# Other buffers for down weights, token tiles and forget gates, and a later place for the queries' weight splits, in a hybrid decoder layer

## The chip, the cores and the metric

The kernel runs on one core of one Trainium2 chip. The metric is the device time of one execution in microseconds; the median of the runs counts. The engines of the core are TensorE (PE in the profile, its weight loads PEld), VectorE (DVE), ScalarE (ACT), GpSimd (POOL) and SyncE (SP), on whose queue all the DMAs named here are issued. Each engine runs its instructions in the order in which they stand in its queue.

## The reference

One layer of a decoder trunk over 1024 tokens with 1024 channels, float32 in and out. Cut to what matters:

```python
x = x + 0.5 * swiglu(rms_norm(x, ffn1_norm), ffn1_w_gate, ffn1_w_up, ffn1_w_down)   # hidden 2816
h = rms_norm(x, mix_norm)
(q_lat, kv_lat, k_rope, fq, fk, fv, f_logit, g_mla, g_fox) = split(h @ w_in)
y_mla = mla_mixer(q_lat, kv_lat, k_rope, ...)           # low-rank latents, rotary key, 8 heads
log_f = log_sigmoid(f_logit + b_f); c = cumsum(log_f)   # forget gates of the 8 FoX heads
y_fox = blocked_causal_attention(norm(fq), norm(fk), fv, bias=c[t] - c[s])
mixed = sigmoid(g_mla + b0) * (y_mla @ w_branch_mla) + sigmoid(g_fox + b1) * (y_fox @ w_branch_fox)
x = x + mixed @ w_o
x = x + 0.5 * swiglu(rms_norm(x, ffn2_norm), ffn2_w_gate, ffn2_w_up, ffn2_w_down)
```

## The kernel before

Matrix products run on PE in float16 with each operand split into a high and a low part, and three products in place of one (hi*hi, hi*lo, lo*hi). The split is made by `split_sb`: ACT writes the high part (L165), DVE the low part (L166). Nearly every operand that PE reads has gone through these two lines.

Both FFNs use a scheme of seven products for a 2x2 block product. In the **up projection** (`ffn_up`, matmuls at L1010) the 22 columns of 128 of the hidden layer are done as two first tiles and then pair tiles, numbered up to 21; POOL makes sums of the weights and activations (L985 to L999, L1060), and after each odd pair `act_sums` (POOL, L826) makes the sums of activations that the down projection needs, which go to DRAM (`sumd`, written at L830). The **down projection** (`ffn_down`, matmuls at L1169 into `psd`) has 70 steps n = (c, i, k): two halves c, seven products i, and CK = 5 blocks k each. A step's operands are prepared three steps ahead by `prep`: it reads the activations' sum back from DRAM (L1109), splits it and the weight (L165, L166), and for four of the products POOL first makes a difference of weight blocks (`made`, L1141: t1, t2, t3, t4). The weight blocks are loaded by `down_load` (L914). `load_x` (L508) loads the eight token tiles to which the result is added; DVE adds it when PSUM is evicted (L1177). `pending` is the `act_sums` of the last pair; it is called at step n = 2*CK.

Behind FFN1 the **tail** (`tail(t)`, called during the end of FFN1's down projection and after it) takes token tile by token tile: normalise it (y, L597), transpose it on PE (L604), split it into high and low (L612 on ACT, L625 on DVE), and project it onto the latents (`lat`, 360 columns: MLA's latents and the forget logits), which are written to DRAM (`latd`, L1299). Then comes the **in-projection** (`in_proj`, `proj_steps`): FoX q, k and v in three groups of weights of 1024x512, each loaded in four pieces by `in_weights` (L1280, into the two buffers `stgi`) and split (L165 to `s_wd`, L166 to `s_act`). Steps of MLA's projections and of the forget gates stand between the tiles. For q and k, `fox_qk` normalises each tile over heads (L1366 to L1371) and transposes it (`psft`, L1376). `forget` loads the logits from `latd` (`fg`, L1397), adds the bias `fb` (L1400), takes the log sigmoid and the running sum, and writes the sums split into high and low (`chl`, L1443 and L1444) to DRAM (`ad` and `bd`, L1446). Its tiles come from the ring of buffers with the tag `stg`, of which there are two and to which `stgi` belongs as well.

Big buffers come from a pool with four tags: 8 slots `u`, and 4 each of `v`, `act` and `wd`. A slot can be written again once its last reader is done, and a load stands on SP's queue until then, with all that is behind it. A scheduler sets the order of instructions on each engine from the program's order and its own costs; `follow` ties an instruction to one that must stand ahead of it in the order.

Of the kernel before, what the change touches and what calls it, by code (L numbers as in the profile page):

```python
# [18 lines left out]
P = 128  # L19
# [45 lines left out]
class Layer:  # L65
# [93 lines left out]
    def split_sb(self, hi, lo, src, scale=None):  # L159
# [4 lines left out]
        else:  # L164
            self.nc.scalar.activation(hi, src, AF.Copy, scale=scale)  # L165
            self.nc.vector.scalar_tensor_tensor(  # L166
                out=lo, in0=src, scalar=scale, in1=hi, op0=ALU.mult, op1=ALU.subtract
            )

# [88 lines left out]
    def layer(self):  # L258
# [18 lines left out]
        def tail(t):  # L277
# [9 lines left out]
            if t >= 1:  # L287
                for f in held.pop(0):
                    f()
            if t >= 2:  # L290
                self.lat_tile(lat["w"], mix, t - 2)
# [3 lines left out]
        x = self.parts("act", NT, 2)  # L295
        mix["x"] = x
        self.ffn_down(x, src, "ffn1", dict(raw=("u", "u"), extra="v", acts="wd", both=("v", "v")), tail, pending)
# [8 lines left out]
        self.in_proj(hT, gates)  # L306
# [453 lines left out]
    def up_tiles(self, norm, name, tags, loads, stats, scales, sumd):  # L760
# [4 lines left out]
        def tile(j, ops, tok, finish, mid):  # L765
# [7 lines left out]
            if j % 2:  # L773
                then = lambda a=box["even"], b=e, k=j // 2 - 1: self.act_sums(a, b, sumd[:, :, k, :], j == NH - 1)
# [300 lines left out]
    def ffn_down(self, x, old, name, tags, tail, pending):  # L1075
# [15 lines left out]
        def weights(k):  # L1091
            if k >= KT or k in raw:
                return
            w = self.down_load(name, k, self.slot(tags["raw"][k % 2]))
# [30 lines left out]
        def prep(n):  # L1125
# [13 lines left out]
            if i in made:  # L1139
                o, u, v = (w[s] for s in made[i])  # L1140
                nc.gpsimd.tensor_tensor(out=o, in0=u, in1=v, op=ALU.subtract)  # L1141
                if (c, i) == (0, 1):
                    second.append(self.latest(mybir.EngineType.Pool))
                if (c, i) == (0, 3):
                    self.follow(second[-1])
# [3 lines left out]
        second = []  # L1149
        mx = self.psa("mx")  # L1150
        ready = [prep(n) for n in range(ahead)]
        self.load_x(x, old, range(NT), loaded[1] if name == "ffn1" else None)
        for n, (c, i, k) in enumerate(steps):
# [8 lines left out]
            if n == 2 * CK:  # L1162
                pending()
# [100 lines left out]
    def in_weights(self, name, c0):  # L1264
# [7 lines left out]
        for kk in range(KD // 2):  # L1272
# [9 lines left out]
            self.split_sb(h, l, st, scale)  # L1282
# [18 lines left out]
    def in_proj(self, hT, gates):  # L1301
# [14 lines left out]
        with self.in_order(mybir.EngineType.PE):  # L1316
            self.proj_steps(hT, gates, groups, due, stages)

    def proj_steps(self, hT, gates, groups, due, stages):
        nc = self.nc  # L1320
        for h in range(2 * 3 * NT):
            gi, t, half = h // (2 * NT), h // 2 % NT, h % 2
            name, c0 = groups[gi]
            if t == 0 and half == 0:
                w = self.in_weights(name, c0)
# [63 lines left out]
    def forget(self):  # L1389
# [4 lines left out]
        w = self.ring.tile([P, 8, N], F32, tag="stg", bufs=2, name="fg")  # L1394
# [25 lines left out]
        to = self.ring.tile([P, 2, P], F32, tag="stg", bufs=2, name="tri")  # L1420
# [9 lines left out]
        ones = self.ring.tile([HEADS, T], F32, tag="stg", bufs=2, name="ones")  # L1430
# [4 lines left out]
        for n in range(2):  # L1435
# [4 lines left out]
            for sgn, dst, r0 in ((1.0, self.ad, 0), (-1.0, self.bd, 1)):  # L1440
                both = self.ring.tile([HEADS, 2, HALF], F32R, tag="stg", bufs=2, name="chl")
# [576 lines left out]
```

## Time and profile before

| | |
|---|---|
| time, three runs | 2097.16, 2098.95, 2099.48 us (median 2098.95) |
| profiled execution | 2101.86 us |
| its span | 2100.0 us, granted TensorE clock 0.992 on the mean |
| PE busy | 2049.2 us, 98% |
| DVE busy | 1445.1 us, 69% |
| ACT busy | 1171.3 us, 56% |
| POOL busy | 647.8 us, 31% |

In the rows of a timeline the first number is the start in us from the start of the span, the second the duration, then engine, line, operation, output<-input, shape and count; in brackets stands the idle time of the engine just ahead of it, and what ended it. FFN1's up projection ends at about 442 us, its down projection at about 640, the tail at 699, the in-projection's q, k and v at about 890; FFN2's down projection starts at about 1888.

### The profile page before, as it was taken

To read this page: it belongs to the slowest core of one execution; us is meant where nothing else is said; L and a number is where in the kernel's file an instruction comes from. 1 tells how busy PE (TensorE), PEld (TensorE's weight loads), DVE (VectorE), ACT (ScalarE), POOL (GpSimd) and SP (SyncE) were. 2 spreads that over 40 slices of the span, in tenths; PEclk is the share of its full clock that TensorE was granted. 3 is DMA by queue.
4 is the path that set the end of the run, shared out by engine and by line. 5 is a ranking of instruction groups with operands and counts; after the bars stand their busy time and mean duration, and the time that the engine had idled before them with its cause. 6 is when DMAs were issued, how large, how long until landed. Compare 5 with 4: busy or idle time off the path is not lost.

```text
span 2100.0 us, 28674 instructions
## 1 busy us (share of the span) xinstructions
PE 2049.2 (98%) x10239; PEld 1160.6 (55%) x10239; DVE 1445.1 (69%) x2421; ACT 1171.3 (56%) x1970; POOL 647.8 (31%) x719
## 2 busy tenths in 40 slices
PE   7999999999999998999999999999999999999999
PEld 4444444444446564567776668888544444444445
DVE  7856666679877776656667777864765555459886
ACT  7666665545554544456666765422566666554552
POOL 2455544463200111112222222000154555555300
PEclk9999999999999999999999999999999999999999
DMA  8258675365434456675555674551454564355432
GB/s 226 75 160 267 209 235 156 140 235 183 139 120 162 138 172 202 205 190 141 145 143 143 185 211 134 181 170 61 121 151 141 170 191 135 121 206 191 141 107 113
DMA packets 275288, 342.02 MB, mean 163 GB/s; under 512 B 20921, under 2 KB 205097, under 8 KB 275146
## 3 DMA queue, kind: packets, MB, share of 16 engines
q1 hardware_dynamic: 275146, 340.21, 52.5%
q8 instruction: 80, 1.31, 0.3%
q14 instruction: 62, 0.51, 0.1%
HBM read 242.15 MB, written 98.00 MB: 162 GB/s over the span
## 4 chain that ended last, share of the span: by engine, by line
PE 83%; DVE 8%; DMA 4%; ACT 3%; issue 2%; SPq 0%; POOL 0%; DVEq 0%; ACTq 0%; POOLq 0%
PE pst L1010 18%; PE psd L1169 15%; PE psb L1010 10%; PE psg L1010 3%; PE pss L1801 3%; PE pspt L1827 3%; PE psb L157 2%; PE psb L155 2%; PE psb L156 2%; PE pspv L1838 2%; PE psgate L155 2%; PE psgate L156 2%; PE psgate L157 2%; DVE op L166 2%; PE psin L156 1%
## 5 line engine op out<-in xcount | busy, mean ns | idle before, releaser
L1010 PEld LDWEIGHTS <-op 128*128 128x128 f16 x3360 | 328.7, 98 | 389.9 <-DVE s_act L1058 1.8
L1169 PE MATMUL psd<-op 128*128 128x512 f16 x1680 | 368.8, 382 | 8.9 <-DVE op L166 8.5
L1169 PEld LDWEIGHTS <-op 128*128 128x128 f16 x1680 | 165.2, 98 | 211.1 <-issue 11.0
L166 DVE SCALAR_TENSOR_TENSOR op<-s_u,s_v,op 128x512 f16<-128x512 f32 x170 | 150.1, 892 | 89.8 <-ACT op L165 89.3
L165 ACT ACTIVATE op<-s_u,s_v 128x512 f16<-128x512 f32 x170 | 118.0, 715 | 88.5 <-PE psd L1169 77.9
L1010 PE MATMUL pst<-s_u,op 128*128 128x512 f16 x720 | 165.2, 379 | 1.3 <-DVE s_act L1058 1.3
L1010 PE MATMUL pst<-s_v,op 128*128 128x512 f16 x720 | 165.2, 379 | 1.3 <-DVE s_u L1058 1.3
L1808 ACT ACTIVATE s_act<-pss,nm 128x128 f32<-128x128 f32 (+7 forms) x128 | 94.9, 742 | 95.1 <-DVE nm L1805 94.7
L166 DVE SCALAR_TENSOR_TENSOR op<-s_act,s_wd,op 128x512 f16<-128x512 f32 x100 | 91.7, 933 | 58.2 <-ACT op L165 58.2
L1848 POOL COPY atp<-cmb 64x128 f32<-64x128 f32 x64 | 18.4, 287 | 331.5 <-DVE cmb L1846 331.5
L1801 PE MATMUL pss<-s_wd 96*128 96x256 f32 (+5 forms) x480 | 115.1, 363 | 1.1 <-DMA s_wd<-mk 1.1
L985 POOL TENSOR_TENSOR sums<-s_u 128x512 f32<-128x512 f32 x20 | 25.8, 1291 | 252.6 <-PE psa L604 158.2
L1831 DVE TENSOR_TENSOR s_v<-pspt,s_v 128x512 fp32r<-128x512 f32 (+1 forms) x160 | 96.1, 631 | 9.9 <-ACT s_v L1830 8.5
L155 PE MATMUL psgate<-s_u,whi 128*128 128x512 f16 x256 | 97.6, 381 | 0.7 <-ACT z L1650 0.5
L157 PE MATMUL psgate<-s_u,wlo 128*128 128x512 f16 x256 | 97.1, 379 | 0.4 <-DVE wlo L166 0.4
L156 PE MATMUL psgate<-s_u,whi 128*128 128x512 f16 x256 | 97.1, 379 | 0.0
L165 ACT ACTIVATE op<-s_wd 128x512 f16<-128x512 f32 x70 | 50.1, 721 | 82.5 <-PE psd L1169 78.4
L1805 DVE TENSOR_REDUCE nm<-pss 128x1 f32<-128x128 f32 (+7 forms) x128 | 93.9, 751 | 1.6
L1830 ACT CAST s_v<-pspt 128x512 fp32r<-128x512 f32 (+1 forms) x160 | 81.3, 545 | 22.7 <-PE pspt L1827 21.3
L1827 PE MATMUL pspt<-ident,s_act 128*128 128x128 f32 x576 | 89.8, 278 | 3.7 <-ACT s_act L1808 2.5
L1846 DVE TENSOR_TENSOR cmb<-pspv,cmb 64x512 f32<-64x512 f32 x64 | 44.0, 688 | 69.8 <-ACT cmb L1845 69.3
L1010 PE MATMUL psb<-s_wd,op 128*128 128x512 f16 x360 | 82.6, 379 | 0.0
(550 smaller groups left out, 4664.6 us busy)
## 6 DMA issues: line engine op xcount, KB each, us to landing
sumd<-s_u SPq DMA_DIRECT2D x20, 1024.0 KB
s_wd<-in_ffn_w_down_dram SPq DMA_DIRECT2D x32, 512.0 KB
s_u<-in_w_in_dram SPq DMA_DIRECT2D x15, 1024.0 KB
sumd<-s_wd SPq DMA_DIRECT2D x13, 1024.0 KB
s_wd<-fd SPq DMA_DIRECT2D x48, 256.0 KB
s_u<-in_ffn_w_down_dram SPq DMA_DIRECT2D x22, 512.0 KB
s_wd<-sumd SPq DMA_DIRECT2D x14, 768.0 KB
s_u<-sumd SPq DMA_DIRECT2D x14, 768.0 KB
```

The lines of the kernel that those rows point to most:

```text
L155: mm(out, lhsT=lh, rhs=rh, start=start, stop=False)
L156: mm(out, lhsT=lh, rhs=rl, start=False, stop=False)
L157: mm(out, lhsT=ll, rhs=rh, start=False, stop=stop)
L165: self.nc.scalar.activation(hi, src, AF.Copy, scale=scale)
L166: self.nc.vector.scalar_tensor_tensor(out=lo, in0=src, scalar=scale, in1=hi, op0=ALU.mult, op1=ALU.subtract)
L1010: mm(out, lhsT=a[:, k, :], rhs=b[:, k, :], start=start and k == 0 and i == 0, stop=k == n - 1 and i == 2, skip_group_check=True,)
L1169: nc.tensor.matmul(o, lhsT=u[:, r], rhs=w, start=start and m == 0, stop=k == CK - 1 and m == 2, skip_group_check=True,)
L1801: mm(ps[:, b:e], lhsT=a[:, q], rhs=bb[:, b:e], start=k == 0, stop=k == len(passes) - 1)
L1805: nc.vector.tensor_reduce(out=nm, in_=ps[:, :n], op=ALU.max, axis=AX.X, negate=True)
L1808: nc.scalar.activation(pn[:, :n], ps[:, :n], AF.Exp, bias=nm, accum_out=rs[:, i, j:j + 1])
L1827: nc.tensor.transpose(pt[:, o:o + P], pr[m][:, kt * P:(kt + 1) * P], self.ident)
L1831: nc.vector.tensor_tensor(out=lo, in0=pt[:, s0:], in1=hi, op=ALU.subtract)
```

## The change

Five parts. (1) FFN1's ten down weight blocks go into `act` slots (0 to 3, 8 and 9; the up projection's weight pairs use these) and `u` slots (4 to 7) in turn, where they all used `u`; the token tiles of FFN1's down projection go into `u` slots, where the norm's output was, and not `act`; they are loaded behind weight block 4 and not behind block 1. (2) In both FFNs the rule that held the first t3 behind the last t2 on POOL is gone. (3) In FFN2 the last pair's `act_sums` are called at n = CK in place of 2*CK, without the tie on their last operation. (4) The splits of q's weights are tied behind the tail's tile 5 on ACT and DVE. (5) `forget` has its tiles in two `u` slots and not in the `stg` ring.

```diff
@@ split_sb
-    def split_sb(self, hi, lo, src, scale=None):
+    def split_sb(self, hi, lo, src, scale=None, after=()):
...
             self.nc.scalar.activation(hi, src, AF.Copy, scale=scale)
+            if after:
+                self.follow(after[0])
             self.nc.vector.scalar_tensor_tensor(
                 out=lo, in0=src, scalar=scale, in1=hi, op0=ALU.mult, op1=ALU.subtract
             )
+            if after:
+                self.follow(after[1])
@@ the program's order: tail, FFN1's down projection, in-projection
+            if t == 5:
+                lat["mark"] = [self.latest(e) for e in (mybir.EngineType.Activation, mybir.EngineType.DVE)]
...
-        x = self.parts("act", NT, 2)
+        x = self.parts("u", NT, 2)
...
-        self.ffn_down(x, src, "ffn1", dict(raw=("u", "u"), extra="v", acts="wd", both=("v", "v")), tail, pending)
+        self.ffn_down(x, src, "ffn1", dict(raw=("act",) * 4 + ("u",) * 4 + ("act",) * 2, extra="v", acts="wd", both=("v", "v")), tail, pending)
...
-        self.in_proj(hT, gates)
+        self.in_proj(hT, gates, lat["mark"])
@@ the up projection's last pair
-                then = lambda a=box["even"], b=e, k=j // 2 - 1: self.act_sums(a, b, sumd[:, :, k, :], j == NH - 1)
+                then = lambda a=box["even"], b=e, k=j // 2 - 1: self.act_sums(
+                    a, b, sumd[:, :, k, :], j == NH - 1 and name == "ffn1"
+                )
@@ ffn_down
-            w = self.down_load(name, k, self.slot(tags["raw"][k % 2]))
+            w = self.down_load(name, k, self.slot(tags["raw"][k % len(tags["raw"])]))
...
-                if (c, i) == (0, 1):
-                    second.append(self.latest(mybir.EngineType.Pool))
-                if (c, i) == (0, 3):
-                    self.follow(second[-1])
...
-        second = []
...
-        self.load_x(x, old, range(NT), loaded[1] if name == "ffn1" else None)
+        if name == "ffn2":
+            self.load_x(x, old, range(NT))
...
-            if n == 2 * CK:
+            if n == 1 and name == "ffn1":
+                self.load_x(x, old, range(NT), loaded[CK - 1])
+            if n == (2 * CK if name == "ffn1" else CK):
                 pending()
@@ in_weights and proj_steps
-    def in_weights(self, name, c0):
+    def in_weights(self, name, c0, after=()):
...
-            self.split_sb(h, l, st, scale)
+            self.split_sb(h, l, st, scale, after)
...
-                w = self.in_weights(name, c0)
+                w = self.in_weights(name, c0, mark if gi == 0 else ())
@@ forget
-        w = self.ring.tile([P, 8, N], F32, tag="stg", bufs=2, name="fg")
+        room, parts = self.slot("u"), self.slot("u", F32R)
+        w = room[:, :8 * N].rearrange("p (k n) -> p k n", k=8)
...
-        to = self.ring.tile([P, 2, P], F32, tag="stg", bufs=2, name="tri")
+        to = room[:, 8 * N:8 * N + 2 * P].rearrange("p (k n) -> p k n", k=2)
...
-        ones = self.ring.tile([HEADS, T], F32, tag="stg", bufs=2, name="ones")
+        ones = room[:HEADS, T:]
...
-            for sgn, dst, r0 in ((1.0, self.ad, 0), (-1.0, self.bd, 1)):
-                both = self.ring.tile([HEADS, 2, HALF], F32R, tag="stg", bufs=2, name="chl")
-                hi, lo = both[:, 0], both[:, 1]
+            for k, (sgn, dst, r0) in enumerate(((1.0, self.ad, 0), (-1.0, self.bd, 1))):
+                hi, lo = (parts[:HEADS, (2 * k + h) * HALF:(2 * k + h + 1) * HALF] for h in range(2))
```

How this moves instructions, at three places. SP's queue where FFN1's up projection goes over into the down projection, before (`sumd` is the sums' DRAM tensor, `s_u`, `s_act` and `s_wd` are slots by their tag):

```order
L830 DMA sumd_105<-s_u 128x4x512 x2
L934 DMA s_u<-in_w_in_dram 128x8x256
L830 DMA sumd_105<-s_u 128x4x512 x2
L914 DMA s_u<-in_ffn_w_down_dram 128x1024 x6
L508 DMA s_act<-in_x_dram 128x1024 x8
L914 DMA s_u<-in_ffn_w_down_dram 128x1024 x2
L1109 DMA s_wd<-sumd_105 128x1024
L914 DMA s_u<-in_ffn_w_down_dram 128x1024 x2
L1109 DMA s_wd<-sumd_105 128x1536
L1109 DMA s_wd<-sumd_105 128x1024
L1109 DMA s_wd<-sumd_105 128x1536
```

And after:

```order
L922 DMA s_act<-in_ffn_w_down_dram 128x1024
L838 DMA sumd_105<-s_u 128x4x512 x2
L942 DMA s_u<-in_w_in_dram 128x8x256
L922 DMA s_act<-in_ffn_w_down_dram 128x1024 x4
L838 DMA sumd_105<-s_u 128x4x512 x2
L922 DMA s_act<-in_ffn_w_down_dram 128x1024 x3
L922 DMA s_u<-in_ffn_w_down_dram 128x1024 x2
L514 DMA s_u<-in_x_dram 128x1024 x3
L1117 DMA s_wd<-sumd_105 128x1024
L514 DMA s_u<-in_x_dram 128x1024 x5
L1117 DMA s_wd<-sumd_105 128x1536
L1117 DMA s_wd<-sumd_105 128x1024
```

The weight blocks' loads, two to a block, stand among the last pair tiles' loads and writes; the eight token tiles (L508, in the new file L514) stand behind ten of them in place of six, and the first read of the sums (L1109, now L1117) stands among the token tiles.

ACT where v's weights are split, before: the `s_wd<-stgi` rows are v's, and they stand behind nearly all of k's tiles.

```order
L1512 ACTIVATE s_v,ss_7129<-s_v 128x128
L1512 ACTIVATE s_v,ss_7129<-s_v 128x32
L106 ACTIVATE rs_y<-rs_a 128x3
L1366 ACTIVATE qk<-psin,ws 128x512
L1378 ACTIVATE qks<-psft,cols 128x512
L106 ACTIVATE rs_y<-rs_a 128x8
L165 ACTIVATE s_wd<-stgi,ws 128x1024 x3
L1597 ACTIVATE mhi<-psmt,cols 128x512
L1598 ACTIVATE mhi<-psmt 128x256
L1531 CAST lt<-psb 128x384
L165 ACTIVATE s_wd<-stgi,ws 128x1024
L165 ACTIVATE vtf<-psin,ws 128x4x64
```

And after, where rows `s_wd<-stgi` are the splits of k's and v's weights (`s_u<-s_u` are the forget gates):

```order
L165 ACTIVATE s_wd<-stgi,ws 128x1024 x2
L1372 ACTIVATE qk<-psin,ws 128x512
L1384 ACTIVATE qks<-psft,cols 128x512
L1412 ACT_TABLE_LOAD
L1412 ACTIVATE s_u<-s_u 128x64
L106 ACT_TABLE_LOAD
L106 ACTIVATE rs_y<-rs_a 128x8
L1537 CAST lt<-psb 128x384
L165 ACTIVATE s_wd<-stgi,ws 128x1024
L1372 ACTIVATE qk<-psin,ws 128x512
L1384 ACTIVATE qks<-psft,cols 128x512
L165 ACTIVATE s_wd<-stgi,ws 128x1024
```

The row with x2 holds k's last two splits, the two rows behind it v's first two; all this stands among q's first tiles at the start of the in-projection.

DVE at the first tile of q (`ss` is the tile's sum of squares, `fg` and `fb` are the forget logits and bias), before:

```order
L166 SCALAR_TENSOR_TENSOR s_act<-stgi,ws,s_wd 128x1024 x3
L1368 TENSOR_REDUCE ss_5762<-qk 128x8
L105 TENSOR_SCALAR rs_a<-ss_5762 128x8
L105 TENSOR_SCALAR rs_a<-ss_5789 128x3
L166 SCALAR_TENSOR_TENSOR s_act<-stgi,ws,s_wd 128x1024
L1400 TENSOR_TENSOR fg<-fg,fb 128x64
L1402 SCALAR_TENSOR_TENSOR fg<-fg 128x64
L107 SCALAR_TENSOR_TENSOR rs_t<-rs_y 128x8
L107 SCALAR_TENSOR_TENSOR rs_t<-rs_y 128x3
```

And after (the logits are in `s_u`):

```order
L168 SCALAR_TENSOR_TENSOR s_act<-stgi,ws,s_wd 128x1024 x2
L1407 TENSOR_TENSOR s_u<-s_u,fb 128x64
L1409 SCALAR_TENSOR_TENSOR s_u<-s_u 128x64
L1374 TENSOR_REDUCE ss_5762<-qk 128x8
L105 TENSOR_SCALAR rs_a<-ss_5762 128x8
L105 TENSOR_SCALAR rs_a<-ss_5789 128x3
L1411 TENSOR_SCALAR s_u<-s_u 128x64
L107 SCALAR_TENSOR_TENSOR rs_t<-rs_y 128x8
L107 SCALAR_TENSOR_TENSOR rs_t<-rs_y 128x3
```

The add of the forget bias and the operation behind it have moved ahead of the first tile's sum of squares.

More of the change, by code (lines that the diff above doesn't have):

```diff
@@ L1299, in lat_tile, with in_proj @@
         self.nc.sync.dma_start(self.latd[t], la)
-    def in_proj(self, hT, gates):
+    def in_proj(self, hT, gates, mark):
         nc = self.nc
@@ L1316, in in_proj, with proj_steps @@
         with self.in_order(mybir.EngineType.PE):
-            self.proj_steps(hT, gates, groups, due, stages)
-    def proj_steps(self, hT, gates, groups, due, stages):
+            self.proj_steps(hT, gates, groups, due, stages, mark)
+    def proj_steps(self, hT, gates, groups, due, stages, mark):
         nc = self.nc
```

## The prediction

> **What bounds the kernel now.** I read the page's busy shares first, then its chain that ended last.
>
> ```profile
> PE 2049.2 (98%) x10239; PEld 1160.6 (55%) x10239; DVE 1445.1 (69%) x2421; ACT 1171.3 (56%) x1970; POOL 647.8 (31%) x719
> PE 83%; DVE 8%; DMA 4%; ACT 3%; issue 2%; SPq 0%; POOL 0%; DVEq 0%; ACTq 0%; POOLq 0%
> ```
>
> PE is busy 2049.2 of 2100.0 us. The change leaves every matmul where it was, so it can win only from the 50.8 us in which PE idles, and from stretches in which PE runs at a lower clock. The view of waits, for PE alone, says for whom PE waited (us, times, longest):
>
> ```profile
> PE psa L604 <- DVE y L597: 8.5, 5, 3.9
> PE psd L1169 <- DVE op L166: 8.5, 5, 4.1
> PE psin L155 <- ACT s_wd L165: 6.8, 2, 5.9
> PE psin L156 <- DVE s_act L166: 2.5, 3, 1.3
> PE psb L155 <- ACT s_u L612: 2.5, 2, 1.3
> PE pst L1010 <- DVE s_act L1058: 1.3, 1, 1.3
> PE psb L157 <- DVE s_u L625: 1.5, 2, 0.7
> ```
>
> Rows two to five and the last are the places that the change touches; the up projection's pair tiles (L1010) hardly wait. The timeline of PE places the five waits of the down projection, four in FFN1 and one in FFN2 (in brackets: idle before, releaser; FFN1's fourth, of 0.20, is not shown):
>
> ```profile
> 453.93 3.40 PE L1169 MATMUL psd<-op 128*128 128x512 f16 x15 [0.79 <-DVE op L166]
> 461.40 12.29 PE L1169 MATMUL psd<-op 128*128 128x512 f16 x45 [4.07 <-DVE op L166]
> 477.24 32.97 PE L1169 MATMUL psd<-op 128*128 128x512 f16 x152 [0.60 <-DVE op L166]
> 1912.28 27.96 PE L1169 MATMUL psd<-op 128*128 128x512 f16 x121 [2.85 <-DVE op L166]
> ```
>
> A matmul takes 32.97 / 152 = 0.217 us in the third row. The 45 of the second should take 9.8 us and took 12.3: 2.5 us lost to the clock. The 121 of the last should take 26.3 and took 28.0: 1.7 lost. Windows show that clock, and who was full (PE, PEld, DVE, ACT, POOL busy, then granted clock, DMA share, GB/s):
>
> ```profile
> 450.00:500.00 50.00, 44.34 (x194) 19.47 (x193) 49.54 (x53) 22.78 (x35) 39.07 (x23) 0.93 0.58 209
> 460.00:462.00 2.00, 0.60 (x2) 0.28 (x3) 2.00 (x3) 0.00 (x0) 2.00 (x2) 0.50 0.02 4
> 695.00:697.00 2.00, 2.00 (x9) 1.06 (x7) 1.87 (x9) 2.00 (x9) 0.00 (x0) 0.50 1.05 403
> 1885.00:1911.00 26.00, 24.43 (x116) 11.30 (x114) 23.47 (x24) 13.17 (x20) 25.41 (x17) 1.00 0.74 254
> 1914.00:1916.00 2.00, 2.00 (x6) 0.73 (x5) 2.00 (x2) 0.06 (x1) 2.00 (x3) 0.50 0.81 285
> ```
>
> DVE has no free time from 450 to 500 while POOL runs 23 operations. And POOL is why DVE is full: the same split of 128x512 on DVE, beside a working POOL and beside an idle one:
>
> ```profile
> 470.42 1.75 DVE L166 SCALAR_TENSOR_TENSOR op<-s_wd,op 128x512 f16<-128x512 f32 x1
> 478.44 0.74 DVE L166 SCALAR_TENSOR_TENSOR op<-s_wd,op 128x512 f16<-128x512 f32 x1
> ```
>
> So each POOL operation of this stage costs DVE about 1.0 us. POOL runs them so late because its weights came late. SP stood 17.79 us on the down weights' u slots, eight token tiles came next, and POOL waited:
>
> ```profile
> 411.33 17.79 SPq L914 DMA_DIRECT2D s_u<-in_ffn_w_down_dram  x6
> 429.16 4.24 SPq L508 DMA_DIRECT2D s_act<-in_x_dram  x8
> 438.63 0.33 SPq L1109 DMA_DIRECT2D s_wd<-sumd  x1
> 446.36 1.28 POOL L1141 TENSOR_TENSOR s_u<-s_u 128x512 f32<-128x512 f32 x1 [4.92 <-DMA s_u<-in_ffn_w_down_dram]
> ```
>
> **A, FFN1's down weights: -7.** They now go into act slots that the pair tiles free one by one, so SP asks for weight 0 about four pair tiles before the end and for 1 to 4 before the token tiles. POOL's first differences (L1141) of weights 0 to 4 can run inside the up projection. Of the 19 POOL operations that I count from 446 to 477, the order of after leaves some 12; 7 fewer at 1.0 us give DVE 7 us back. All there is to win is 0.79 + 4.07 + 0.20 + 0.60 + 2.5 = 8.2. Bounds -8.2 and -4 (DVE gets back only what the longest wait was). The cover is POOL's free time in the up projection, where PE lost 1.3 us in the row above; if POOL is held there by a weight's second half, it delays a scale on ACT by some us. I cost that at nothing, since 1.3 is all that PE lost there, and at up to +2 in the bound of -4.
>
> **B, v's weights in the in-projection: -11.** Forget's last tiles (chl) held both buffers of the ring that v's weight loads use, so those were asked for only at 815 to 826, behind chl's writes:
>
> ```profile
> 804.87 0.62 SPq L1446 DMA_DIRECT2D bd<-chl  x2
> 818.43 7.60 SPq L1280 DMA_DIRECT2D stgi<-in_w_in_dram  x3
> 819.92 1.15 ACT L165 ACTIVATE s_wd<-stgi,ws 128x1024 f16<-128x1024 f32 x1 [1.61 <-DMA stgi<-in_w_in_dram]
> 821.12 0.59 PE L155 MATMUL psin<-s_wd,s_u 128*128 128x512 f16 x1 [5.88 <-ACT s_wd L165]
> 832.94 0.38 PE L156 MATMUL psin<-s_act,s_u 128*128 128x512 f16 x1 [1.28 <-DVE s_act L166]
> 826.00:828.00 2.00, 2.00 (x7) 0.50 0.56 142
> 828.00:830.00 2.00, 2.00 (x14) 0.97 0.33 121
> ```
>
> The waits for s_wd and s_act, 6.8 + 2.5 = 9.3 us, are all v's. The last two rows (PE's windows) show 7 matmuls in 2 us at half clock and 14 at full; 11 matmuls ran at half clock between 821 and 828, 0.215 us too long each: 2.4 more. Together 11.7. With forget in u slots, the order has all eight loads of k and v in one row behind q's, some 90 us ahead of their use. I take 11, bounds -9 and -12.5. Forget's two slots are free there: only its own steps use them.
>
> **C, start of the tail: -2.** ACT met q's split ahead of the cast that PE waited for:
>
> ```profile
> 649.41 1.15 ACT L165 ACTIVATE s_wd<-stgi,ws 128x1024 f16<-128x1024 f32 x1 [2.38 <-DMA stgi<-in_w_in_dram]
> ```
>
> ACT stands 2.38 us on the load and 1.15 on the split; half of the waits for hi and lo (L612 2.5, L625 1.5) are here, 2.0. Behind t = 5 the splits delay nothing here. Bounds 0 (the tail's start waits for DVE's evictions anyway) and -2.6 (with a share of the first row's waits for y).
>
> **D, end of the tail: -0.5.** There the four splits arrive (ACT 1.15 each, DVE 1.28 each by the row below). The other half of the hi and lo waits, 2.0, and about 1.8 us of half clock (window 695 to 697) come from this:
>
> ```profile
> 691.05 0.62 ACT L1497 CAST s_v<-stgm 128x512 fp32r<-128x512 f32 x1 [4.19 <-DMA stgm<-in_mla_w_kvb_dram]
> 703.90 1.28 DVE L166 SCALAR_TENSOR_TENSOR s_act<-stgi,ws,s_wd 128x1024 f16<-128x1024 f32 x1 [3.81 <-ACT s_wd L165]
> ```
>
> Only one of the two kvb casts is left ahead of the last tile's cast: -0.6. On DVE two splits stand ahead of the next norm tile (y): 2.6 us, of which PE sees what goes beyond the time that y is ready early; of the 8.5 us of waits for y the longest, 3.9, lies at the start of the program, so I take that as covered. Bounds -2.5 (the kvb wait is hidden behind the splits) and +2 (y uncovered); I take -0.5.
>
> **E, start of the in-projection: +3.** This is what the change costs. Before and around the first tile of q stood:
>
> ```profile
> 705.22 0.37 SPq L1397 DMA_DIRECT2D fg<-latd  x1
> 705.28 0.69 DVE L1368 TENSOR_REDUCE ss<-qk 128x8 f32<-128x512 f32 x1
> 707.52 0.22 DVE L1400 TENSOR_TENSOR fg<-fg,fb 128x64 f32<-128x64 f32 x1
> 708.92 0.69 DVE L1371 TENSOR_TENSOR qk<-psin,rs_y 128x512 f32<-128x512 f32 x1
> 709.75 0.63 PE L1376 MATMUL psft<-ident,qk 128*128 128x128 f32 x4
> 716.73 0.63 PE L1376 MATMUL psft<-ident,qk 128*128 128x128 f32 x4 [0.85 <-DVE qk L1371]
> ```
>
> Now forget's add (fb) stands on DVE ahead of that reduce, and it waits for the load asked for at 705.22, which needs all eight lat tiles written. Here the add ran at 707.52. The reduce then starts at about 707.9, 2.6 us later, qk is scaled at 711.5 instead of 708.92, and PE, whose transpose at 709.75 came 0.14 us after qk's end (708.92 + 0.69), waits 2.4 us; I add 0.6 for the clock and v's splits that now share ACT and DVE with the first tiles (four more of each: 4.6 and 5.1 us in a stretch with little slack, as the 0.85 shows). Bounds 0 (the load lands sooner) and +8 (three tiles in a row late, and half clock between them).
>
> On the clock: after 2.85 us of idle (1912.28) the granted clock was 0.50 in 1914 to 1916, and after two idles of 1.3 and 0.7 it was 0.50 at 695. The Trainium skill (TensorE: Matmul & The Clock Gate, HAM oscillation) says that only idle gaps over about 3.4 us drop the clock. By that rule E would be +2.4 and the forecast 2077.8; the trace differs, and decides.
>
> **F, FFN2's down projection: -3.** POOL is full from 1885 to 1911 (25.41 of 26), as in A. The wait of 2.85 and 1.7 for the clock are all there is: 4.55. Without the rule that held the t3 differences behind all t2 ones, POOL makes them one by one earlier, and the last pair's sums (pending) are five steps earlier; but the latter's writes stand on SP ahead of a load of summed activations. Bounds 0 and -4.55; -3, nearer to A's share.
>
> **Sum.** -7 -11 -2 -0.5 +3 -3 = -20.5. The profiled execution took 2101.86 us (span 2100.0) and would take 2081.4; it stands 2.9 above the median of 2098.95, so against the runs shown 2078.
>
> **Rivals.**
> First: the in-projection's start costs +12. Every tile of q there goes PE, ACT, DVE, ACT, DVE, PE; if forget's step and v's splits push several of them, PE idles over 2 us each time and falls to half clock. For: the 0.85 row, no slack. Against: v's splits are 5 us of work on each engine, in a stretch of 100 (716 to 815). Time 2078.4 + 9 = 2087.
> Second: the down projections stay bound by DVE (A and F give 2 instead of 10), because POOL's work is moved into DVE's busy time and not out of it. For: DVE 23.47 of 26 in 1885 to 1911. Against: the up projection hardly waits. Time 2086.
> Third, slower: the token tiles, now in u slots, hold SP's queue. If one waits for the last pair's sums on POOL, the load of summed activations behind it (438.63 before) comes after about 462 and not before 442, and PE waits some 24 us at the border: 2078.4 + 7 + 24 = 2109. It decides from a wait of 17.7 us (13.5 of the other gains and 4.2). Against: the order puts that load behind the third token tile, and those slots belong to earlier pairs.
> Fourth, no change: v's loads are early but its splits end up between the first tiles' steps with E at +12, and SP's row leaves v late for half of its tiles; B gives nothing: 2078.4 + 11 + 9 = 2098.
>
> **Chances and range.** Forecast 0.61, first 0.15, second 0.12, third 0.05, fourth 0.07. Within 0.2% (4.2 us, about what a measurement of this kernel can tell) is the fourth; slower is the third; faster is the rest, 0.88. The bounds that gain most add up to -30.4, 2068.5; with the 2.9 between executions 2066. At the top, the first two rivals with a spread of 5: 2092.
>
> **What would show it.** Right: no PE wait over 1 us on psd in 442 to 480 and DVE splits of 0.74 there; no PE wait on s_wd or s_act of v; a PE wait of 1 to 3 us on psft at the in-projection's start. Wrong: PE waiting on sumd's loads at the border, several waits on psft or psin after the tail, or POOL as full as before at FFN2's border.

## The result, and the profile after

The changed kernel takes 2082.61 us (median of four runs, 2079.29 to 2085.40) where the kernel before takes 2098.43 (2097.16 to 2099.48, four runs): the ratio is 0.9924, with a 95% interval of 0.9907 to 0.9941, or 15.8 us faster. The forecast was 2078, range 2066 to 2092. The profiled execution took 2079.29 (span 2077.2), 22.6 less than the one of before.

The page's busy times and its chain that ended last:

```profile
PE 2044.1 (98%) x10239; PEld 1160.7 (56%) x10239; DVE 1432.0 (69%) x2421; ACT 1170.1 (56%) x1970; POOL 645.9 (31%) x719
PE 83%; DVE 8%; DMA 3%; ACT 2%; issue 2%; POOL 1%; SPq 0%; DVEq 0%; ACTq 0%; POOLq 0%
```

PE's busy time is 5.1 us shorter with the same 10239 matmuls, since fewer of them ran at half clock, and PE idles 33.1 us in place of 50.8. For whom PE waited (us, times, longest); the lines of the new file are some 2 to 8 higher:

```profile
PE psa L610 <- DVE y L603: 5.5, 4, 2.8
PE psmt L1597 <- DVE s_v L1586: 3.2, 2, 2.9
PE psb L1018 <- ACT s_u L1051: 2.1, 1, 2.1
PE psd L1175 <- DVE op L168: 1.8, 3, 1.4
PE psft L1382 <- DVE s_u L1419: 1.7, 1, 1.7
PE psb L157 <- DVE s_u L631: 0.7, 1, 0.7
```

The waits for v's weights (6.8 + 2.5) are gone, that on the down projections' splits is 1.8 in place of 8.5. Rows two and three are new. Row five was 0.8 before; the profile names L1419, a step of the gates that ended last ahead of it, but the tile that PE transposes there was done by L1377 at 709.29, 0.15 us before PE started. At the start of the two down projections PE's timeline has only this left:

```profile
468.85 13.11 PE L1175 MATMUL psd<-op 128*128 128x512 f16 x60 [1.43 <-DVE op L168]
1904.22 26.06 PE L1175 MATMUL psd<-op 128*128 128x512 f16 x120 [0.20 <-DVE op L168]
```

The windows (PE, PEld, DVE, ACT, POOL busy, clock, DMA share, GB/s) show why, first before, then after, then after at FFN2's border, where PE's sequence is 18.5 us early (the window of before is the prediction's, 1885 to 1911):

```profile
446.00:476.00 30.00, 24.57 (x102) 10.38 (x101) 28.94 (x26) 13.29 (x20) 28.86 (x19) 0.89 0.65 240
```

```profile
446.00:476.00 30.00, 28.57 (x136) 13.19 (x134) 28.93 (x35) 14.90 (x23) 17.94 (x13) 1.00 0.73 254
1866.50:1892.50 26.00, 26.00 (x124) 12.05 (x122) 23.95 (x28) 13.17 (x20) 19.57 (x14) 1.00 0.65 241
```

POOL runs 13 operations in the 30 us where it ran 19, DVE is as full as before but gets 35 instructions done in place of 26, and PE 136 matmuls in place of 102. Of DVE's splits into `op` that start in these 30 us, 14 of 22 take some 0.74 us, where before it was 1 of 16. At FFN2's border POOL runs 14 operations where it ran 17, and is busy for 19.57 us in place of 25.41.

To see where the time went, I take each piece of PE's sequence, which is the same in both kernels, and subtract its start before from its start after. The table gives by how much that difference grew in each stage (us, + is lost, always against the profiled execution of before; columns are bounded by the times of before). The experiments of the next section are in it too.

| | up proj. 385-410 | FFN1 down | tail start 633-660 | tail end 690-703 | in-proj. start 703-745 | rest of q, k 745-815 | v 815-840 | gates 889-912 | FFN2 down | all |
|---|---|---|---|---|---|---|---|---|---|---|
| changed | +3.9 | -7.5 | -3.1 | -2.5 | +4.0 | -0.5 | -12.8 | +2.0 | -4.2 | -22.7 |
| a1_changed_again | +2.4 | -7.4 | -1.8 | -2.5 | +4.3 | -0.5 | -12.8 | +1.6 | -4.2 | -23.1 |
| e1_gates_in_ring | +2.5 | -7.5 | -2.3 | -3.0 | +1.4 | 0.0 | -1.3 | -0.2 | -4.2 | -14.5 |
| e2_only_gates | 0.0 | -0.3 | +0.2 | -1.8 | +4.9 | -0.5 | -12.8 | +0.2 | -0.2 | -13.3 |
| e3_only_slots | +0.6 | -4.9 | +6.3 | -1.3 | +1.7 | 0.0 | -1.0 | -0.1 | -0.4 | -1.0 |
| e4_t2_behind_pair | +0.3 | -7.5 | -2.9 | -3.1 | +5.5 | -0.5 | -12.8 | -0.2 | -4.2 | -26.4 |
| e5_q_splits_free | +2.6 | -7.5 | +3.8 | -1.7 | +5.6 | -0.5 | -12.8 | 0.0 | -4.2 | -13.9 |
| e6_ffn2_sums_late | +2.4 | -7.5 | -2.3 | -2.6 | +4.0 | -0.5 | -12.8 | +1.7 | -2.2 | -20.1 |
| e7_gates_later | +3.9 | -7.5 | -2.2 | -2.4 | +6.9 | +1.1 | -12.8 | +0.3 | -4.5 | -18.7 |
| e9_three_ties | +0.1 | -7.5 | -2.1 | -2.6 | +1.6 | +4.1 | -12.8 | -0.2 | -4.5 | -25.9 |
| e10_v_splits_together | +0.3 | -7.4 | -2.2 | -3.0 | +0.9 | +3.1 | -12.8 | -0.1 | -4.2 | -26.4 |
| e12_v_splits_spread | 0.0 | -7.5 | -2.2 | -2.7 | +1.4 | +3.5 | -12.5 | +0.2 | -4.2 | -24.7 |
| e13_ffn2_rule_back | +0.9 | -6.2 | -2.0 | -2.9 | +4.0 | -0.5 | -12.8 | 0.0 | -1.9 | -23.0 |

What is missing to "all" lies in the first 60 us (-0.3 to +1.3) and in the attention (+0.4 to -3.0 from 950 to 1400). The latter comes in kernels that touch nothing near it too (e3: -2.9), so it belongs to the profiled execution of before, which was 3.4 us above the median, and not to the change: there PE waited 2.06 us at 1287.47 and then ran at half clock for 3.41 us. Of the others only e1 and e5 lost the clock there, and they gain least (-0.9 and +0.4). Two profiled executions of the changed kernel differ by 1.5 at most in any column.

The two columns with a new loss, in the trace of after. The up projection, on SP, POOL, ACT and PE:

```profile
371.23 4.63 SPq L838 DMA_DIRECT2D sumd<-s_u  x2
...
376.46 33.09 SPq L922 DMA_DIRECT2D s_act<-in_ffn_w_down_dram  x4
```

```profile
386.27 1.27 POOL L1149 TENSOR_TENSOR s_v<-s_act 128x512 f32<-128x512 f32 x1 [8.46 <-DMA s_act<-in_ffn_w_down_dram]
387.61 1.27 POOL L1149 TENSOR_TENSOR s_v<-s_v,s_act 128x512 f32<-128x512 f32 x1
...
392.64 1.27 POOL L1068 TENSOR_TENSOR s_u<-s_u 128x512 f32<-128x512 f32 x1
```

```profile
393.94 1.06 ACT L915 ACTIVATE s_wd<-s_u 128x1024 bf16<-128x1024 f32 x1 [7.13 <-POOL s_u L1068]
```

```profile
398.89 4.37 PE L1018 MATMUL psb<-s_u,op 128*128 128x512 f16 x12 [2.12 <-ACT s_u L1051]
```

POOL stands 8.46 us on the second half of weight block 0, which SP issues behind the sums' writes and a load; all that the pair tile needs of POOL stands behind that and behind the next difference, t3 (387.61). L1068 runs at 392.64, where the same product (L1060) ran at 385.81 before; ACT's L915 waits 7.13 for it, and PE 2.12. The 12 matmuls of the last row take 4.37 us where 12 take 2.75: 1.6 more went to the clock.

And the in-projection's start, on DVE and on PE:

```profile
694.24 2.65 DVE L168 SCALAR_TENSOR_TENSOR s_act<-stgi,ws,s_wd 128x1024 f16<-128x1024 f32 x2 [4.42 <-ACT s_wd L165]
697.20 0.22 DVE L1407 TENSOR_TENSOR s_u<-s_u,fb 128x64 f32<-128x64 f32 x1 [0.31 <-DMA s_u<-latd]
...
697.60 0.68 DVE L1374 TENSOR_REDUCE ss<-qk 128x8 f32<-128x512 f32 x1
...
716.90 1.28 DVE L168 SCALAR_TENSOR_TENSOR s_act<-stgi,ws,s_wd 128x1024 f16<-128x1024 f32 x1 [0.23 <-ACT s_wd L165]
...
719.36 1.28 DVE L168 SCALAR_TENSOR_TENSOR s_act<-stgi,ws,s_wd 128x1024 f16<-128x1024 f32 x1 [0.16 <-ACT s_wd L165]
```

```profile
709.44 0.63 PE L1382 MATMUL psft<-ident,qk 128*128 128x128 f32 x4 [1.66 <-DVE s_u L1419]
```

```profile
724.33 0.63 PE L1597 MATMUL psmt<-ident,s_v 128*128 128x128 f32 x4 [2.91 <-DVE s_v L1586]
```

The gates' add does stand ahead of the first reduce, but it waits only 0.31 us for its load: DVE was held up to 696.9 by two splits of k's weights anyway, and PE waits 0.48 us for this tile. The 1.66 is at q's second tile. The greatest wait, 2.91, comes later, at the first MLA tile, with the last two of v's splits (716.90 and 719.36) in DVE's row ahead of it.

### The profile page after: what moved, and what is told of

Same layout as the page of the kernel before. It is cut to its first block, busy times and chain, and to the rows that moved or that the text cites. A ratio compares the mean times of both kernels' runs of the same rounds, so it can differ in the third digit from the quotient of the medians.

```text
span 2077.2 us, 28670 instructions
## 1 busy us (share of the span) xinstructions
PE 2044.1 (98%) x10239; PEld 1160.7 (56%) x10239; DVE 1432.0 (69%) x2421; ACT 1170.1 (56%) x1970; POOL 645.9 (31%) x719
## 4 chain that ended last, share of the span: by engine, by line
PE 83%; DVE 8%; DMA 3%; ACT 2%; issue 2%; POOL 1%; SPq 0%; DVEq 0%; ACTq 0%; POOLq 0%
PE pst L1018 18%; PE psd L1175 14%; PE psb L1018 10%; PE pss L1807 4%; PE psg L1018 3%; PE pspt L1833 3%; DVE op L168 3%; PE pspv L1844 3%; PE psgate L155 2%; PE psgate L156 2%; PE psgate L157 2%; PE psb L157 2%; PE psb L156 2%; PE psb L155 2%; PE psin L155 1%
## 5 line engine op out<-in xcount | busy, mean ns | idle before, releaser
L1175 PE MATMUL psd<-op 128*128 128x512 f16 x1680 | 364.2, 379 | 1.8 <-DVE op L168 1.8
L168 DVE SCALAR_TENSOR_TENSOR op<-s_act,s_wd,op 128x512 f16<-128x512 f32 x130 | 122.3, 953 | 61.0 <-ACT op L165 60.9
L165 ACT ACTIVATE op<-s_act,s_wd 128x512 f16<-128x512 f32 x130 | 88.8, 710 | 8.6 <-PE pst L1018 4.1
```

What stands on the lines that cost most here:

```text
L168: self.nc.vector.scalar_tensor_tensor(out=lo, in0=src, scalar=scale, in1=hi, op0=ALU.mult, op1=ALU.subtract)
L1175: nc.tensor.matmul(o, lhsT=u[:, r], rhs=w, start=start and m == 0, stop=k == CK - 1 and m == 2, skip_group_check=True,)
```

## Experiments

Two theories were against each other at each place: that every part of the change works by the local wait that the profile shows, and a rival named with each run. Ratios are to the kernel before on the same chip, with 95% intervals.

**The gates' tiles back in the ring.** The changed kernel, with

```diff
-        room, parts = self.slot("u"), self.slot("u", F32R)
-        w = room[:, :8 * N].rearrange("p (k n) -> p k n", k=8)
+        w = self.ring.tile([P, 8, N], F32, tag="stg", bufs=2, name="fg")
```

and the same for `tri`, `ones` and `chl`.

> The changed kernel with the forget gates' tiles back in the stg ring; all else stays changed. Theory (each part works at its own place): v's weights come late again, PE waits 9 us on s_wd and s_act of v and loses 2 to 3 us to the clock, while the 4 us that the in-projection's start lost come back: 8 to 9 us slower than the changed kernel, about 2091. Rival (v's late weights were a matter of traffic on SP's queue, which the earlier loads of parts 1 to 4 have already cleared): v's weights stay early, and the time is that of the changed kernel or 4 us less.

2086.61 us (2085.09 to 2090.20), ratio 0.9944 (0.9931 to 0.9956). v's weights come late again; SP and PE:

```profile
795.80 0.83 SPq L1452 DMA_DIRECT2D bd<-chl  x2
...
810.23 6.85 SPq L1286 DMA_DIRECT2D stgi<-in_w_in_dram  x3
```

```profile
812.63 0.59 PE L155 MATMUL psin<-s_wd,s_u 128*128 128x512 f16 x1 [5.58 <-ACT s_wd L165]
```

In the table, v's column falls from -12.8 to -1.3 and the in-projection's start from +4.0 to +1.4: 8.9 us net between the profiles, as expected. The medians, of different chips, differ by 4.0 to 5.0 only. The rival is out: traffic on SP was not it, the ring was.

**The gates' tiles alone.** The kernel before with these same lines changed and nothing else.

> The kernel before with nothing but the forget gates' tiles moved to u slots. Theory: 12 us at v are won, and at the in-projection's start some 2 to 4 are lost to v's splits and the gates' steps among q's first tiles: 8 to 10 us faster than before, about 2089. Rival (the loss at the start comes from the queries' splits that part 4 moved, not from the gates): no loss there, 12 us faster, about 2086.

2088.69 us (2087.89 to 2090.41), ratio 0.9953 (0.9940 to 0.9967): 10.1 faster. v gains 12.8; the in-projection's start loses 4.9 though the queries' splits stand where they stood and the gates' add, in this kernel's order, stands behind the first reduce. So neither of these two is what that start loses to.

**The slots alone.** The kernel before with part 1 (the tags of `raw`, `parts("u", NT, 2)`, `load_x` behind block 4).

> The kernel before with part 1 alone: FFN1's down weights in act and u slots, token tiles in u slots, loaded behind block 4. Theory: FFN1's down projection starts without its 8.2 us of waits and clock, and the up projection loses 3.8 near 400 us: 4 to 5 us faster than before, about 2094. Rival (the tail's gain of 3 to 5 us came with the token tiles' place and not with the queries' splits): 8 to 9 us faster, about 2090.

2100.88 us (2097.79 to 2105.73), ratio 1.0009 (1.0000 to 1.0018): a miss. The down projection's start gains 4.9 and the tail loses 6.3; some 4 of these are the clock, which was 0.50 for 10.24 us behind the wait below. Waits of PE, and its row in the tail:

```profile
PE psd L1172 <- DVE op L166: 5.2, 2, 2.9
```

```profile
643.69 1.17 PE L604 MATMUL psa<-ident,y 128*128 128x128 f32 x8 [2.65 <-DVE y L597]
```

Both sides of the expectation were wrong: with part 1 the tail starts worse, not better, as long as the queries' splits stand at its start. Which of part 1's three pieces does that was not run apart. What part 1 wins in the down projection stays won as a whole only together with part 4.

**The queries' splits free.** The changed kernel without part 4: `w = self.in_weights(name, c0)`.

> The changed kernel without part 4: the queries' splits stand where the scheduler puts them. Theory (these splits hold ACT and DVE at the tail's start): the tail loses the 3 to 4 us that it had won at its start and 2 to 3 at its end, and since part 1 alone lost 6 us in the tail, up to 8 to 10 in all; the gates' add goes behind the first reduce again, which gives 1 back. 7 us slower than the changed kernel, about 2089. Rival (the tail's gain came from the token tiles' slots): within 2 us of the changed kernel.

2086.34 us (2083.07 to 2089.21), ratio 0.9934 (0.9921 to 0.9947), 4.7 slower than the changed kernel on the same chip (2081.60, below). The tail's start loses 3.8 where the changed kernel gains 3.1. PE and ACT:

```profile
643.22 3.70 PE L610 MATMUL psa<-ident,y 128*128 128x128 f32 x16 [3.55 <-DVE y L603]
```

```profile
640.34 1.15 ACT L165 ACTIVATE s_wd<-stgi,ws 128x1024 f16<-128x1024 f32 x1 [1.51 <-DMA stgi<-in_w_in_dram]
...
645.37 1.15 ACT L165 ACTIVATE s_wd<-stgi,ws 128x1024 f16<-128x1024 f32 x1 [3.70 <-DMA stgi<-in_w_in_dram]
```

ACT stands 1.51 us on a load of q's weights and 1.15 on its split ahead of the root (L119, at 641.39) that this y waits for, and then 3.70 on the next load with the tail's casts behind it. The theory holds, at a lower price by the medians than by the profile. The in-projection's start loses 5.6, with the gates' add behind the first reduce in this kernel: a second sign that the add is not the cause.

**The changed kernel again**, unaltered.

> The changed kernel once more, unaltered, on the chip of the next three. Its profiled execution lost 3.5 us at the up projection's wait near 399; the kernel with t2 of block 0 tied was 7.7 us faster by the medians. Theory (POOL stands on a transfer there, and a transfer's end varies): the wait is longer in another execution, 4 to 8 us with the clock, and the median is again 2081 to 2084. Rival (the difference of medians is one of chips): the wait is again 2.1 us, and the median is within 2077 to 2080.

2081.60 us (2078.88 to 2083.02), ratio 0.9907 (0.9894 to 0.9921). The median is in the theory's range, but the wait is shorter, not longer:

```profile
PE psb L1018 <- ACT s_u L1051: 1.8, 1, 1.8
```

So the wait varies (its column is +2.4 to +3.9 in the six profiled executions with POOL's order of the change there, with +3.9 where the clock fell behind the wait and 2.4 to 2.6 where it did not), and why most executions without a profile are 3 us and more above the profiled one is not settled.

**t2 behind the pair.** The changed kernel with one tie on POOL:

```diff
         nc.gpsimd.tensor_tensor(out=e[:, 1], in0=e[:, 1], in1=e[:, 2], op=ALU.mult)
+        self.muls = getattr(self, "muls", []) + [self.latest(mybir.EngineType.Pool)]
...
                 nc.gpsimd.tensor_tensor(out=o, in0=u, in1=v, op=ALU.subtract)
+                if name == "ffn1" and (c, i, k) == (0, 1, 0):
+                    self.follow(self.muls[-4])
```

> The changed kernel with one tie more: POOL's t2 of weight block 0 stands behind the pair tile's product of sums (L1068), so that POOL does not stand on the block's second half ahead of it. Theory (POOL's queue was held): the PE wait of 2.1 us near 399 and the half clock behind it go, 3.5 to 4 us faster than the changed kernel, about 2079. Rival (the earlier weight loads take bandwidth from the pair tiles' loads and sums): the wait stays within 0.5 us, no change in time.

2074.90 us (2073.06 to 2075.55), ratio 0.9885 (0.9871 to 0.9898): the fastest of all kernels run. The up projection's column is +0.3. On POOL and ACT:

```profile
386.52 1.71 POOL L1068 TENSOR_TENSOR s_u<-s_u 128x512 f32<-128x512 f32 x1
388.19 1.27 POOL L1150 TENSOR_TENSOR s_v<-s_act 128x512 f32<-128x512 f32 x1
```

```profile
389.69 1.06 ACT L915 ACTIVATE s_wd<-s_u 128x1024 bf16<-128x1024 f32 x1 [2.85 <-DVE s_u L1076]
```

The same loads are issued at the same time (the second half of block 0 at 376.46 and here at 376.50), only their reader waits behind the pair tile's product instead of ahead of it: the queue was the cause, not bandwidth. The medians win 7 us, the profiled executions 3.3 to 3.7. Of the latter 2 are in the column of the gates, told in the last section; what the medians win beyond that is the difference between executions that is not settled above.

**The gates' chain later.** The changed kernel with

```diff
+        last = self.latest(mybir.EngineType.DVE)
         v.tensor_tensor(out=z3, in0=z3, in1=fb.unsqueeze(1).broadcast_to([P, NT, HEADS]), op=ALU.add)
+        self.follow(last)
```

> The changed kernel with the gates' add tied behind the first tile of k on DVE, so that the whole chain of the gates runs some 35 us later; v's splits stay where they are. Theory (the add ahead of q's first reduce, and the two table loads behind it, are what the in-projection's start lost): 2.5 to 4 of the 4.0 us come back, about 2079. Rival (v's eight splits on ACT and DVE hold q's first tiles): 1 us or less comes back, and PE still waits about 3 us for the first MLA tile near 724.

2081.14 us (2080.40 to 2083.09), ratio 0.9910 (0.9896 to 0.9924): no change. The theory falls, the rival's sign is there; PE at the in-projection's start:

```profile
704.91 0.63 PE L1382 MATMUL psft<-ident,qk 128*128 128x128 f32 x4 [2.66 <-ACT qk L1372]
```

```profile
726.58 0.86 PE L1599 MATMUL psmt<-ident,s_v 128*128 128x128 f32 x4 [3.23 <-DVE s_v L1588]
```

The start loses 6.9 in place of 4.0, without any step of the gates in it. The first wait comes from a split of k's weights, on whose load ACT stands ahead of the first tile's root (`rs_y`, L106); behind the second the clock was 0.50 for 3.41 us:

```profile
700.44 1.15 ACT L165 ACTIVATE s_wd<-stgi,ws 128x1024 f16<-128x1024 f32 x1 [2.60 <-DMA stgi<-in_w_in_dram]
```

**Three ties.** e4 and e7 together, and v's four splits tied behind the tile of k at step 20:

```diff
-                w = self.in_weights(name, c0, mark if gi == 0 else ())
+                w = self.in_weights(name, c0, (mark, (), vmark)[gi])
...
+            if h == 20:
+                vmark = [self.latest(e) for e in (mybir.EngineType.Activation, mybir.EngineType.DVE)]
```

> The changed kernel with three ties: t2 of weight block 0 behind the pair's product, the gates' add behind the first tile of k, and v's four splits behind the tile of k that stands at step 20. Theory: the tie of t2 gives what it gave (2075), and the in-projection's start loses next to nothing: 4 to 5 us less, about 2070.5. Rival (the splits and the gates' chain only move their cost to k's tiles, or v comes late again): 2074 or more.

2078.90 us (2075.89 to 2080.78), ratio 0.9898 (0.9883 to 0.9913): the rival holds. The start falls to +1.6, but k's tiles go from -0.5 to +4.1, where the splits and the gates' chain now stand:

```profile
768.29 0.66 PE L1388 MATMUL psft<-ident,qk 128*128 128x128 f32 x4 [1.31 <-DVE qks L1391]
...
786.92 0.63 PE L1388 MATMUL psft<-ident,qk 128*128 128x128 f32 x4 [1.65 <-DVE rs_y L109]
```

**v's splits tied, the gates where they were.** As e9 without the tie of the gates (e10), and with one split each behind the tiles at steps 14, 18, 22 and 26 (e12):

```diff
-            self.split_sb(h, l, st, scale, after)
+            self.split_sb(h, l, st, scale, after[kk] if len(after) == 4 else after)
...
-            if h == 20:
-                vmark = [self.latest(e) for e in (mybir.EngineType.Activation, mybir.EngineType.DVE)]
+            if h in (14, 18, 22, 26):
+                vmark += ([self.latest(e) for e in (mybir.EngineType.Activation, mybir.EngineType.DVE)],)
```

> The changed kernel with t2 of block 0 tied as before and v's four splits tied behind the tile of k at step 20; the gates stay where the change has them. Theory (v's splits among q's first tiles are what the in-projection's start lost, since with the gates moved away and the splits left there it lost 6.9 us, and with both moved 1.6): the start loses 1 to 2 us, k's tiles some 2 to 3 for the four splits in a row: about 2074, within 2 us of the kernel with t2 tied alone. Rival (the gates' add ahead of the first reduce is the loss): the start loses 4 us or more.

> As the kernel before it, but v's four splits tied one by one behind the tiles at steps 14, 18, 22 and 26, so that no two meet in one tile. Theory (a tile's chain over PE, ACT and DVE has room for one split of 1.2 us, not for two): 1 to 2 us at the start, under 1 us after it: 3 to 4 us faster than with t2 tied alone, about 2071. Rival (each split costs PE about the same wherever it stands): 2074 to 2076.

e10: 2075.87 us (2073.97 to 2076.55), ratio 0.9882 (0.9866 to 0.9898). e12: 2076.70 (2075.72 to 2077.61), ratio 0.9887 (0.9868 to 0.9905). In e10 the start loses 0.9, with the gates' add ahead of the first reduce: v's splits were most of what it lost to (PE still waits 1.36 us at q's second tile). But k's tiles lose 3.1, so nothing is won over e4. Spreading them does not help: +1.4 and +3.5, and its theory falls. PE, e10:

```profile
766.96 0.63 PE L1388 MATMUL psft<-ident,qk 128*128 128x128 f32 x4 [1.19 <-DVE qk L1383]
781.31 0.63 PE L1603 MATMUL psmt<-ident,s_v 128*128 128x128 f32 x4 [1.98 <-DVE s_v L1592]
```

And e12:

```profile
745.72 0.59 PE L1541 MATMUL psb<-ident,s_v 128*128 128x128 f32 x3 [1.73 <-DVE s_v L1530]
```

Over the two columns of q and k together, e1, without v's splits, loses 1.4; the changed kernel loses 3.5, e4 5.0, e10 4.0 and e12 4.9 (e7 and e9, with the gates' chain among k's tiles, 8.0 and 5.7). So v's four splits cost PE 2 to 4 us wherever they stand among these tiles, as e12's rival said, and 11.5 where the ring put them.

**FFN2's two edits apart.** The changed kernel with the last sums of FFN2 late again (e6):

```diff
-                    a, b, sumd[:, :, k, :], j == NH - 1 and name == "ffn1"
+                    a, b, sumd[:, :, k, :], j == NH - 1
...
-            if n == (2 * CK if name == "ffn1" else CK):
+            if n == 2 * CK:
```

and with the rule of t3 behind t2 back (e13, the four lines of `second`).

> The changed kernel with FFN2's last act_sums called at 2*CK again, and tied again; the rule of t3 behind t2 stays gone. Theory (the t3 differences are what POOL had late, so the rule's removal is what wins at FFN2's start): the 4.2 us stay, no change against the changed kernel, about 2082. Rival (the earlier sums are what wins): PE waits 2.9 us again and loses the clock, 4 us slower, about 2086.

> The changed kernel with the rule back that puts the first t3 behind the last t2 on POOL, in both FFNs; FFN2's last sums stay early. With the rule gone and the sums late, 2.2 of the 4.2 us at FFN2's start were left. Theory (the two parts add up): 2 us stay won there, PE waits about 1.5 us, and FFN1's start is as with the rule gone: about 2 us slower than the changed kernel. Rival (the early sums alone win all 4.2): no PE wait there, no change.

e6: 2082.52 us (2080.18 to 2084.76), ratio 0.9915 (0.9897 to 0.9932). e13: 2083.54 (2079.25 to 2087.52), ratio 0.9929 (0.9905 to 0.9953). Two us are too little for these intervals, so the profiles decide; PE in e6, then in e13:

```profile
1893.31 5.34 PE L1175 MATMUL psd<-op 128*128 128x512 f16 x24 [1.79 <-DVE op L168]
```

```profile
1890.99 39.23 PE L1180 MATMUL psd<-op 128*128 128x512 f16 x181 [2.67 <-DVE op L168]
```

With the sums late 2.2 of the 4.2 us stay, with the rule back 1.9: each edit gives about half, where e6's theory and rival both gave all of it to one. e13's theory holds there, but not in FFN1: the rule's removal gives 1.3 in its down projection (-6.2 against -7.5). And it costs more than that ahead of it: with the rule back, which changes the order on POOL alone, the up projection loses 0.9 in place of 2.4 to 3.9 (e3, which has the rule too: 0.6). POOL stands on the same half of block 0 for 8.45 us, but the first t3 does not follow it, and the pair tile's product runs 1.6 us sooner; POOL and PE in e13:

```profile
391.06 1.27 POOL L1068 TENSOR_TENSOR s_u<-s_u 128x512 f32<-128x512 f32 x1
```

```profile
397.32 2.75 PE L1018 MATMUL psb<-s_u,op 128*128 128x512 f16 x12 [0.75 <-ACT s_u L1051]
```

So in FFN1 the rule's removal wins nothing on balance by these profiles (-5.3 in the two columns with the rule, -3.6 and -5.0 in the changed kernel), unless t2 is tied as in e4 (-7.2).

## Why the prediction was right, and where not

The sum of the forecast was -20.5 against the profiled execution of before, and -22.7 came; by medians it was -15.8 and, on another chip, -19.0. That the profiles come so near is in part luck: the +3.9 and +2.0 of the up projection and the gates were in no term and E was 1.0 short, 6.9 in all, while A, B, C, D and F gave 6.6 more than was forecast; and 3.0 lie in the attention, where the profiled execution of before lost the clock. By its steps:

- A, -7: the down projection gave -7.5, by fewer POOL operations under DVE's splits, as worked out (13 in place of 19 where I counted on 12). What failed is the sentence "I cost that at nothing" on the cover in the up projection: POOL's free time there was no cover, since an in-order queue hands a wait on to all that stands behind it (8.46 us on POOL, 7.13 on ACT, 2.12 on PE). It cost +2.4 to +3.9, over the +2 of the bound. The row of 1.3 us that it went by is a wait at 1538.98, in FFN2; in FFN1's up projection before, PE's one wait on L1010 was 1.28 at 89.49, and none was near 399, which told nothing of the slack once POOL stood still. e4 shows it and takes it away. Part 2 has its share: without the first t3 in that place the loss is 0.9 (e13).
- B, -11: -12.8, and e1 and e2 tie it to the ring. The bound of -12.5 was 0.3 short.
- C, -2, and D, -0.5: -3.1 and -2.5 (-1.8 and -2.5 the second time); C's bound of -2.6 was 0.5 short. C's mechanism held (e5), but part 1 had raised its stake: alone it would have lost 6.3 in the tail (e3). I treated the parts as adding up; two of them do not. D came out at its bound's end; -1.3 to -1.8 of it come without part 4 too, in e2, e3 and e5: before lost the clock there (0.50 from 695.00 to 698.41, after waits of 1.32 and 0.73), and e5, with waits of 1.28 and 0.73, did not. So most of D is the clock of the one execution that was profiled before, and not the splits' place.
- E, +3: +4.0, near in size by luck and wrong in cause. The step that failed is "the reduce then starts at about 707.9, 2.6 us later": the add waited 0.31 us, and PE 0.48 at that tile where 2.4 was worked out. The loss is 1.66 at the second tile and 2.91 at the first MLA tile; the clock, for which E had a share of 0.6, stayed at 1.00. Of the two causes named, the one priced at 2.4, the gates' add, costs at most 0.9 (e10), and the one priced as part of 0.6, v's splits, is most of the rest: moving them away brought the start from 4.0 to 0.9 (from 5.5 in e4, which lost the clock as well), moving the add away gave nothing (e7). A place in the order says who stands ahead, not that he is late.
- F, -3: -4.2, all there was, from both edits in about equal parts.
- Not forecast: +2.0 at the gates (889 to 912; +1.6 the second time), where the clock fell; e4, with the same order on PE, ACT, DVE and SP, kept it (last section).

Of the rivals, the first (the start eats +12) named the right engines and the wrong size. The second and the third did not come: POOL's work did leave the down projections, and the first read of the sums was issued at 435.7, ahead of their start. The fourth did not come, as v was early throughout. Of the signs, v's waits are gone and a wait of 1.66 on psft is there, but a wait of 1.43 on psd at 468.85 is above the 1 us that was named, and no sign named psmt, where PE waits longest.

## What to carry to other kernels

When loads are moved earlier, look at who reads them first and what stands behind that reader in its queue: one tie that let the pair tile's own work go ahead of an early difference on POOL was worth 7 us by the medians (3 to 4 between profiled executions), beside 16 for the whole change. Work taken out of a stall is not gone: v's splits, out of an 11.5 us hole, cost 2 to 4 us wherever they were put among tiles whose chain over PE, ACT and DVE has little slack. And parts of a change that each look like a local wait should be run alone where they share a stage; here one part alone was worth nothing, since what it won in one stage it lost in the next, and another part won that back.

## What the runs showed of the hardware

In all fourteen traces the half clock, but for that cut off by the end of the span, lasts 3.41 us or a whole number of times that. Counted on from there, the whole span falls into stretches of 3.41 us, and whether the clock falls goes with how long PE idles inside one of them. Here are, in after, the stretch ahead of 398.89 and the one behind it, then the two over which the longer wait of 724.33 lies and the one behind them (PE, PEld, DVE, ACT, POOL busy, clock, DMA share, GB/s):

```profile
395.38:398.79 3.41, 1.39 (x7) 0.52 (x6) 3.06 (x4) 2.79 (x6) 3.33 (x3) 1.00 0.00 0
398.79:402.20 3.41, 3.31 (x8) 1.13 (x8) 3.17 (x3) 1.86 (x4) 2.58 (x2) 0.50 0.00 0
```

```profile
719.65:723.06 3.41, 1.76 (x9) 0.59 (x6) 3.41 (x11) 2.27 (x10) 0.00 (x0) 1.00 0.85 196
723.06:726.47 3.41, 2.14 (x13) 1.32 (x14) 3.38 (x12) 1.04 (x3) 2.64 (x6) 1.00 1.06 348
726.47:729.88 3.41, 3.41 (x20) 1.79 (x19) 2.93 (x8) 1.28 (x3) 1.20 (x6) 1.00 0.77 224
```

The wait of 2.12 us lies nearly whole in one stretch, which idles 2.02 us, and costs 1.6 more; the wait of 2.91 is cut into 1.65 and 1.27 by a border and costs nothing more. In e4 nearly the same wait, 3.04 at 720.46, lies for the most part in one stretch, and the in-projection's start loses 5.5 in place of 4.0, with the other waits there the same:

```profile
716.47:719.88 3.41, 0.95 (x5) 0.22 (x3) 3.41 (x12) 1.58 (x8) 0.68 (x2) 1.00 0.70 160
719.88:723.29 3.41, 2.83 (x10) 1.63 (x11) 3.38 (x12) 1.04 (x3) 1.96 (x5) 0.50 1.02 342
```

From 20 us on and but for the last 8, all 18 stretches at full clock that idle 2.02 us or more are followed by half clock, and none that idles under 1.49; between these 6 of 37 lost the clock, and what decides there is not shown. The gates are such a place: the changed kernel and e4 run the same instructions there, but after idles 1.55 us in one stretch and loses the clock, which is the 2 us of the column, and e4 idles 1.46 and keeps it.

```profile
883.49:886.90 3.41, 1.86 (x10) 1.11 (x9) 0.76 (x4) 0.78 (x1) 0.00 (x0) 1.00 1.05 316
886.90:890.31 3.41, 3.41 (x9) 1.24 (x9) 0.29 (x1) 0.92 (x4) 0.00 (x0) 0.50 1.04 236
```

The losses at 398.80 and 886.90 came after less than the 3.4 us that the Trainium skill (TensorE: Matmul & The Clock Gate, HAM oscillation) gives as the gap from which the clock drops; by that rule neither would have come. So a wait of 2 to 3 us counts once or nearly twice by where it lies against these stretches, and that differs between executions of one kernel: at 399 and at the gates the two profiled executions of the change differ by 1.5 and 0.4.
